# Operands of the down projection issued five steps ahead in program order, across changes of product

## The chip, the cores and the metric

The kernel runs on one core of a Trainium2 chip. The metric is the device time of one execution in microseconds (us); the time of a kernel is the median of its timed runs. The profile is of one further execution, whose own time and span are given beside it.

## What is computed

One layer of a hybrid decoder on x of 2048 tokens by 1024 channels, in fp32: a normalised input projection feeds a short convolution and a state-space mixer, an output projection adds their result to x, and an MLP follows. The change touches only the last product of the MLP:

```python
h = _rmsnorm(x, norm_mlp_pre[i])
f = jnp.square(jax.nn.relu(jnp.einsum("btd,df->btf", h, w_up[i])))    # 1024 -> 4096
f = jnp.einsum("btf,fd->btd", f, w_down[i])                           # 4096 -> 1024
x = x + _rmsnorm(f, norm_mlp_post[i])
```

## The kernel before

Every fp32 operand of a matmul is split into a high and a low part, and a product is made of three matmuls: high by high, high by low, low by high. `split` (L495, L496) does this: ACT casts the high part, DVE subtracts it for the low one.

The down projection (`down_stage`) is done in the manner of Strassen: seven products of block sums instead of eight of blocks, in the order 0, 1, 5, 6, 4, 2, 3. Below, "5.3" is step 3 of product 5. Each product runs over 16 steps p of the inner dimension. A step multiplies one tile of weights (128x512) with eight tiles of activations, at eight *sites* (two groups g, four token tiles t). Each site has one PSUM bank, three named "mm" and five "ax", and there are eight banks in all. A step is therefore 8 x 3 = 24 matmuls (L826 to L828), and the first matmul of a product at a site needs the bank that the product before still holds there.

`down_operands(i, p)` issues what a step needs. On SP it loads one to three tiles of w_down into "raw" (L747) or the stored t2 (L744); `less` subtracts them on DVE into "us" (L734); for product 5, whose weight has three parts, the result is also stored to t2 (L753), for product 3 to read. `split` makes "wh" and "wl" of it. For each of the two groups it loads one or two parts of the activations from DRAM into "xt" (L760); where there are two, POOL subtracts them into "fs" (L734, the same helper). `split` puts the high parts into "hh" and "hl" and the low parts into seven homes that are used in turn ("row", "m" for group 0, "bk", "bT", "cT", "scm", "xd", "xdh" for group 1). Buffers: raw 6, us 4, xt 6, fs 4, wh and wl 9 each.

After the 16 steps, `close` takes a product's result out of its banks: an ACT copy for product 0 (L799), an add on DVE for the others (`add`, L791). For products 1, 2 and 3 `half` (ACT square L766, POOL multiply L768, DVE multiply L772) and `finish` (L776 to L783) follow with the normalisation, the sum with x and the store of the output. In the last product the last six steps are kept back and done site by site (LATE).

The program text issues the operands of a step right ahead of the matmuls of that step; the operands of 5.0 so come behind the closes of product 1 in the text. A scheduler of the framework then sets each engine's order, with the place in the text as priority, so that loads and casts run ahead of the text where their buffers allow. An engine works off its own list in order and waits at the head of it.

Of the kernel before, what the change touches and what calls it, by code (L numbers as in the profile page):

```python
# [44 lines left out]
def hybrid_layer(ctx: ExitStack, tc: tile.TileContext, x, xT, w_in, w_dt, w_out, w_up, w_down,  # L45
                 chan, rows, hrow, out):
    nc = tc.nc
    V, S, G, PE, SY = nc.vector, nc.scalar, nc.gpsimd, nc.tensor, nc.sync
# [5 lines left out]
    def big(tag, dt=F32):  # L54
        return sb.tile([P, 512], dt, tag=tag, name=tag, bufs=BUFS.get(tag, 1))

    def bank(tag="ax"):
        return ps.tile([P, 512], F32, tag=tag, name=tag, bufs=BUFS[tag])
# [4 lines left out]
    def cols(n, *dims):  # L63
        size = n
        for d in dims:
            size *= d
        a = cst[:, used[0]:used[0] + size]
        used[0] += size
        assert used[0] <= C_ALL
        return a.rearrange("p (a b) -> p a b", a=n) if dims else a  # L70
# [401 lines left out]
    NP = FF // P // 2  # L472
    NG = T // PB
    B7 = range(7)
    ORDER = (0, 1, 5, 6, 4, 2, 3)
# [3 lines left out]
    t2_d = [dram.tile([P, 512], F32, name=f"t2_{p}") for p in range(NP)]  # L479
# [13 lines left out]
    def split(v, tags):  # L493
        hi, lo = (big(t, F32R) for t in tags)
        S.copy(hi, v)  # L495
        V.tensor_sub(lo, v, hi.bitcast(F32))  # L496
        return hi, lo
# [223 lines left out]
        save("a12", relu2(plus(u3, product(3))), S)  # L721


    LATE = 6
    ROUND = (HOMES[0], HOMES[2][:7]), (HOMES[1], HOMES[3][:7])
    step = [0]

# [4 lines left out]
    def less(eng, tag, a, b):  # L732
        c = big(tag)
        eng.tensor_tensor(c, a, b, op=ALU.subtract)  # L734
        return c

    def down_operands(i, p):
        n = step[0]
        step[0] += 1
        ws = []  # L740
        for at in W_PARTS[i]:
            raw = big("raw")
            if at is None:
                SY.dma_start(raw, t2_d[p])  # L744
            else:
                j, k = at
                SY.dma_start(raw.rearrange("p (a b) -> p a b", a=1),  # L747
                             w_down[2 * p + j][:, k:k + 1, :])
            ws.append(raw)
        v = ws[0] if len(ws) == 1 else less(V, "us", ws[0], ws[1])  # L750
        if len(ws) == 3:
            v = less(V, "us", ws[2], v)
            S.dma_start(t2_d[p], v)  # L753
        w = split(v, ("wh", "wl"))
        f = []
        for g in range(NG):
            fs = []
            for part in F_PARTS[i]:
                fs.append(big("xt"))
                SY.dma_start(fs[-1], f_d[g][p][part])  # L760
            v = fs[0] if len(fs) == 1 else less(G, "fs", *fs)
            f.append(split(v, [r[n % len(r)] for r in ROUND[g]]))
        return f, w

    def half(m, s2, i, first=False):
        S.activation(big("us"), m, AF.Square, accum_out=s2[:, i:i + 1])  # L766
        if first:
            G.tensor_tensor(m, m, gmlp[i], op=ALU.mult)  # L768
            V.tensor_scalar(s2[:, 2:3], s2[:, i:i + 1], 1.0 / D, EPS, op0=ALU.mult, op1=ALU.add)
            return m  # L770
        v = big("fs")
        V.tensor_tensor(v, m, gmlp[i], op=ALU.mult)  # L772
        V.tensor_scalar(s2[:, 3:4], s2[:, i:i + 1], 1.0 / D, s2[:, 2:3], op0=ALU.mult, op1=ALU.add)
        return v

    def finish(m, s2, tok, last):  # L776
        r = cols(1)
        G.tensor_tensor(r, s2[:, 3:4], mhalf[:, :1], op=ALU.pow)
        for i in range(2):
            xt = big("raw" if last else "fs")  # L780
            SY.dma_start(xt, x1_d[tok][:, i * 512:(i + 1) * 512])
            V.scalar_tensor_tensor(xt, m[i], r, xt, op0=ALU.mult, op1=ALU.add)
            (SY if last and i == 0 else S if last else G).dma_start(out[tok * P:(tok + 1) * P, i * 512:(i + 1) * 512], xt)  # L783

    def down_stage():
        sites = [(g, t) for g in range(NG) for t in range(TT)]
        u, w, c, s2 = {}, {}, {}, {}

        def add(dst, a, pt):
            dst = big("acc") if dst is None else dst  # L790
            V.tensor_tensor(dst, a, pt, op=ALU.add)  # L791
            return dst

        def close(i, k, pt):
            g, t = k
            tok = 2 * g * TT + t
            if i == 0:
                u[k] = big("acc")
                S.copy(u[k], pt)  # L799
            elif i == 1:  # L800
                c[k] = add(None, u[k], pt)
                s2[k] = cols(4)
                half(c[k], s2[k], 0, True)
            elif i == 5:
                add(u[k], u[k], pt)
            elif i == 6:
                w[k] = add(None, u[k], pt)
            elif i == 4:
                u[k] = add(u[k], u[k], pt), add(None, w[k], pt)
            elif i == 2:  # L810
                add(u[k][0], u[k][0], pt)
                finish([c[k], half(u[k][0], s2[k], 1)], s2[k], tok, False)
                s2[k] = cols(4)
                half(u[k][1], s2[k], 1, True)
            else:
                add(w[k], w[k], pt)
                finish([half(w[k], s2[k], 0), u[k][1]], s2[k], tok + TT, True)

        for i in ORDER:
            late = LATE if i == ORDER[-1] else 0  # L820
            banks = {k: bank("mm" if n < 3 else "ax") for n, k in enumerate(sites)}

            def mac(p, ops, k):
                (fh, fl), (wh, wl) = ops[0][k[0]], ops[1]
                ts = slice(k[1] * P, (k[1] + 1) * P)
                PE.matmul(banks[k], lhsT=fh[:, ts], rhs=wh, start=(p == 0), stop=False)  # L826
                PE.matmul(banks[k], lhsT=fh[:, ts], rhs=wl, start=False, stop=False)  # L827
                PE.matmul(banks[k], lhsT=fl[:, ts], rhs=wh, start=False, stop=(p == NP - 1))  # L828

            kept = []  # L830
            for p in range(NP):
                ops = down_operands(i, p)
                if p >= NP - late:
                    kept.append((p, ops))
                    continue
                for k in sites:
                    mac(p, ops, k)
                    if p == NP - 1:
                        close(i, k, banks[k])
            for k in sites if kept else ():  # L840
                for p, ops in kept:
                    mac(p, ops, k)
                close(i, k, banks[k])

    raw = up_load(0, 0)
    for g in range(NG):
        hb7 = hidden_blocks(g)
        for p in range(NP):
# [3 lines left out]
            up(g, p, hb7, wb7)  # L852
            drain(1)
    down_stage()


# [39 lines left out]
```

## Time and profile before

| | us |
|---|---|
| timed runs | 2795.24, 2800.82, 2802.17 |
| median | 2800.82 |
| profiled execution | 2797.18 |
| its span | 2795.5 |
| PE busy in it | 2717.7 |

The mean granted clock of TensorE in the profiled execution is 0.987. The span is the time from the first to the last instruction in the trace; 1.7 us of the execution lie outside it. Engines are named PE (matmuls), PEld (weight loads of PE), DVE, ACT, POOL and SP; L826 is line 826 of the kernel. In a timeline, "[8.15 <-ACT wh L495]" says that the engine had stood idle for 8.15 us and that ACT's write of wh in line 495 released it. Records of adjacent matmuls overlap: a matmul of 0.39 us is followed by the next after 0.23.

### The profile page before, as it was taken

What the parts mean: (1) busy time and instruction counts of PE and PEld (TensorE: products, weight loads), DVE (VectorE), ACT (ScalarE), POOL (GpSimd) and SP (SyncE); (2) the same over time, 40 slices, a digit from 0 to 9 for tenths busy, and PEclk for the clock granted to TensorE, in tenths of its full rate; (3) what the DMA queues carried; (4) which work ended last, traced back from release to release, by engine and by line L of the source; (5) the groups of instructions that cost most, each with busy time, mean ns of one, the idle gap of its engine ahead of it and who ended that gap; (6) DMA issues with size and microseconds to landing.
All of it is one profiled execution on the core that took longest, in us unless ns stands there. A gap on an engine that the chain in (4) does not pass through costs nothing.

```text
span 2795.5 us, 37710 instructions
## 1 busy us (share of the span) xinstructions
PE 2717.7 (97%) x12822; PEld 2239.3 (80%) x12822; DVE 1886.4 (67%) x3351; ACT 1353.3 (48%) x2361; POOL 645.3 (23%) x546
## 2 busy tenths in 40 slices
PE   8999999999999999999999999999999999799978
PEld 6888888888888888788887888878888877688867
DVE  6675867767676678677587776886665336665675
ACT  6545545464455455555554565665455323233331
POOL 1111312113221224221121233321221011413330
PEclk9999999999999999999999999999999999999989
DMA  8423334333344325643335556763436438866565
GB/s 276 141 87 117 107 112 147 123 110 98 117 137 139 112 97 182 215 153 113 109 100 168 175 186 213 272 216 140 147 121 222 143 121 293 281 240 215 189 218 186
DMA packets 257521, 456.83 MB, mean 163 GB/s; under 512 B 28080, under 2 KB 44848, under 8 KB 257328
## 3 DMA queue, kind: packets, MB, share of 16 engines
q1 hardware_dynamic: 199184, 361.60, 39.3%
q10 hardware_dynamic: 51744, 71.84, 7.0%
q0 software_dynamic: 6400, 20.98, 1.9%
q8 instruction: 101, 1.65, 0.2%
q14 instruction: 92, 0.75, 0.1%
HBM read 359.81 MB, written 94.50 MB: 163 GB/s over the span
## 4 chain that ended last, share of the span: by engine, by line
PE 55%; DVE 2%; DMA 2%; issue 0%; ACT 0%; POOL 0%; SPq 0%; ACTq 0%; DVEq 0%; POOLq 0%
PE ax L827 4%; PE ax L826 4%; PE ax L828 4%; PE mm L686 3%; PE mm L687 3%; PE mm L688 3%; PE ax L686 3%; PE ax L687 3%; PE ax L688 3%; PE mm L827 3%; PE mm L828 3%; PE mm L826 3%; PE mm L155 3%; PE mm L154 3%; PE mm L156 3%; PE ax L166 1%
## 5 line engine op out<-in xcount | busy, mean ns | idle before, releaser
L154 PE MATMUL mm<-hh,wh 128*128 128x512 f32 x1408 | 555.5, 395 | 4.2 <-ACT hh L143 2.2
L155 PE MATMUL mm<-hl,wh 128*128 128x512 f32 x1408 | 551.0, 391 | 0.6 <-DVE hl L144 0.5
L156 PE MATMUL mm<-hh,wl 128*128 128x512 f32 x1408 | 550.1, 391 | 0.0
L99 DVE TENSOR_TENSOR wl<-raw,wh 128x512 fp32r<-128x512 f32 x480 | 368.2, 778 | 240.6 <-ACT wh L98 229.3
L98 ACT CAST wh<-raw 128x512 fp32r<-128x512 f32 x480 | 293.0, 617 | 464.5 <-PE mm L155 294.4
L154 PEld LDWEIGHTS mm<-hh,wh 128*128 128x128 f32 x1408 | 265.6, 189 | 59.8 <-issue 3.3
L156 PEld LDWEIGHTS mm<-hh,wl 128*128 128x128 f32 x1408 | 265.4, 189 | 55.8
L155 PEld LDWEIGHTS mm<-hl,wh 128*128 128x128 f32 x1408 | 265.5, 189 | 55.4 <-DVE hl L144 2.0
L166 PE MATMUL ax<-wh,yh 128*128 128x512 f32 x512 | 201.1, 393 | 0.0
L168 PE MATMUL ax<-wh,yl 128*128 128x512 f32 x512 | 199.5, 390 | 0.0
L167 PE MATMUL ax<-wl,yh 128*128 128x512 f32 x512 | 199.3, 389 | 0.0
L496 DVE TENSOR_TENSOR wl<-us,wh 128x512 fp32r<-128x512 f32 x192 | 148.5, 777 | 72.5 <-ACT wh L495 42.9
L495 ACT CAST wh<-us 128x512 fp32r<-128x512 f32 x192 | 114.8, 617 | 129.3 <-DVE us L734 60.5
L826 PE MATMUL ax<-wh,hl 128*128 128x512 f32 x448 | 175.0, 391 | 0.0
L827 PE MATMUL ax<-wl,hl 128*128 128x512 f32 x448 | 174.6, 390 | 0.0
L826 PE MATMUL mm<-wh,hh 128*128 128x512 f32 x336 | 132.5, 397 | 39.8 <-ACT wh L495 25.4
L496 DVE TENSOR_TENSOR wl<-raw,wh 128x512 fp32r<-128x512 f32 x99 | 83.4, 846 | 102.3 <-ACT wh L495 59.6
L734 POOL TENSOR_TENSOR fs<-xt 128x512 f32<-128x512 f32 x64 | 94.8, 1489 | 226.5 <-DMA xt<-f_a 94.7
L717 POOL TENSOR_TENSOR fs<-uc 128x512 f32<-128x512 f32 x32 | 42.2, 1320 | 398.3 <-ACT uc L698 203.9
L827 PE MATMUL mm<-wl,hh 128*128 128x512 f32 x336 | 132.8, 395 | 0.7 <-DVE wl L496 0.7
L369 POOL TENSOR_TENSOR row<-row,cT 128x512 f32<-128x512 f32 x60 | 98.9, 1669 | 133.7 <-ACT cT L295 78.0
L697 ACT ACTIVATE uc<-uc 128x512 f32<-128x512 f32 x128 | 80.7, 631 | 101.2 <-DVE uc L693 91.5
(462 smaller groups left out, 6009.3 us busy)
## 6 DMA issues: line engine op xcount, KB each, us to landing
raw<-w_in_dram SPq DMA_DIRECT2D x352, 256.0 KB, 2.8
xt<-f_a SPq DMA_DIRECT2D x192, 256.0 KB, 4.5
raw<-w_down_dram SPq DMA_DIRECT2D x176, 256.0 KB, 4.9
raw<-w_out_dram SPq DMA_DIRECT2D x128, 256.0 KB, 2.8
f_a<-uc ACTq DMA_DIRECT2D x128, 256.0 KB, 2.2
xt<-f_s SPq DMA_DIRECT2D x96, 256.0 KB, 4.1
raw<-w_up_dram SPq DMA_DIRECT2D x68, 256.0 KB, 3.4
row<-cs SPq DMA_DIRECT2D x64, 256.0 KB, 3.9
```

What stands on the lines that cost most here:

```text
L98: S.copy(hi, raw)
L99: V.tensor_sub(lo, raw, hi.bitcast(F32))
L154: PE.matmul(pt, lhsT=wh[:, ks], rhs=ah[k], start=(k == 0), stop=False)
L155: PE.matmul(pt, lhsT=wh[:, ks], rhs=al[k], start=False, stop=False)
L156: PE.matmul(pt, lhsT=wl[:, ks], rhs=ah[k], start=False, stop=(k == KT - 1))
L166: PE.matmul(pts[t], lhsT=a, rhs=wh, start=(i == 0), stop=False)
L167: PE.matmul(pts[t], lhsT=a, rhs=wl, start=False, stop=False)
L168: PE.matmul(pts[t], lhsT=c, rhs=wh, start=False, stop=(i == n - 1))
L496: V.tensor_sub(lo, v, hi.bitcast(F32))
L826: PE.matmul(banks[k], lhsT=fh[:, ts], rhs=wh, start=(p == 0), stop=False)
L827: PE.matmul(banks[k], lhsT=fh[:, ts], rhs=wl, start=False, stop=False)
L828: PE.matmul(banks[k], lhsT=fl[:, ts], rhs=wh, start=False, stop=(p == NP - 1))
```

## The change

A list of all steps in the order of the products is made ahead, and `ready` holds the operands that have been issued. Before the matmuls of a step are issued, operands are issued until six steps (AHEAD + 1) are in `ready`; the step then takes the oldest. So the operands of a step now stand in the text five steps of matmuls earlier, and those of a product's first five steps stand ahead of the closes of the product before. The store of t2 goes from ACT's queue to POOL's. The whole diff:

```diff
--- before.py
+++ after.py
@@ -721,7 +721,7 @@
         save("a12", relu2(plus(u3, product(3))), S)
 
 
-    LATE = 6
+    LATE, AHEAD = 6, 5
     ROUND = (HOMES[0], HOMES[2][:7]), (HOMES[1], HOMES[3][:7])
     step = [0]
 
@@ -750,7 +750,7 @@
         v = ws[0] if len(ws) == 1 else less(V, "us", ws[0], ws[1])
         if len(ws) == 3:
             v = less(V, "us", ws[2], v)
-            S.dma_start(t2_d[p], v)
+            G.dma_start(t2_d[p], v)
         w = split(v, ("wh", "wl"))
         f = []
         for g in range(NG):
@@ -816,6 +816,8 @@
                 add(w[k], w[k], pt)
                 finish([half(w[k], s2[k], 0), u[k][1]], s2[k], tok + TT, True)
 
+        order = [(i, p) for i in ORDER for p in range(NP)]
+        ready = []
         for i in ORDER:
             late = LATE if i == ORDER[-1] else 0
             banks = {k: bank("mm" if n < 3 else "ax") for n, k in enumerate(sites)}
@@ -829,7 +831,9 @@
 
             kept = []
             for p in range(NP):
-                ops = down_operands(i, p)
+                while order and len(ready) <= AHEAD:
+                    ready.append(down_operands(*order.pop(0)))
+                ops = ready.pop(0)
                 if p >= NP - late:
                     kept.append((p, ops))
                     continue
```

Nothing is computed otherwise; the number of loads, subtractions, casts and matmuls is the same. What changes is each engine's order. Three places are shown; a number behind a name counts the tiles of the program, so that the same step has another number before and after.

**DVE at the end of product 1, before.** acc_21709 to acc_21772 are the eight closes of product 1, row_22059 and bT_22065 low parts of activations of product 5, us_21792 the first subtraction for the weight of 5.0.

```order
L496 TENSOR_TENSOR row_22059<-xt_22056,hh_22058 128x512
L496 TENSOR_TENSOR bT_22065<-xt_22062,hl_22064 128x512
L791 TENSOR_TENSOR acc_21709<-acc_21013,mm_21050 128x512
...
L791 TENSOR_TENSOR acc_21772<-acc_21048,ax_21057 128x512
...
L496 TENSOR_TENSOR row_22110<-xt_22107,hh_22109 128x512
...
L734 TENSOR_TENSOR us_21792<-raw_21786,raw_21788 128x512
```

**The same place after the change.** us_21822 and wl_21826 are the weight of 5.4, us_21927 the first subtraction for 5.5; acc_21844 to acc_21907 are the closes.

```order
L734 TENSOR_TENSOR us_21822<-raw_21818,us_21820 128x512
...
L496 TENSOR_TENSOR wl_21775<-us_21771,wh_21774 128x512
L496 TENSOR_TENSOR xdh_21736<-xt_21733,hl_21735 128x512
L496 TENSOR_TENSOR wl_21826<-us_21822,wh_21825 128x512
...
L791 TENSOR_TENSOR acc_21844<-acc_21103,mm_21140 128x512
...
L791 TENSOR_TENSOR acc_21907<-acc_21138,ax_21147 128x512
...
L496 TENSOR_TENSOR row_21990<-xt_21987,hh_21989 128x512
...
L734 TENSOR_TENSOR us_21927<-raw_21921,raw_21923 128x512
```

The weights of 5.0 to 5.4 have moved from behind the closes of product 1 to ahead of them.

**DVE at the end of product 5, before.** us_23000 is the weight of 6.7, us_23054 that of 6.8; acc_21013 and so on are the closes of product 5.

```order
L496 TENSOR_TENSOR wl_22949<-us_22946,wh_22948 128x512
L734 TENSOR_TENSOR us_23000<-raw_22996,raw_22998 128x512
L496 TENSOR_TENSOR m_22959<-fs_22956,hh_22958 128x512
L734 TENSOR_TENSOR us_23054<-raw_23050,raw_23052 128x512
L496 TENSOR_TENSOR scm_22915<-fs_22912,hl_22914 128x512
L791 TENSOR_TENSOR acc_21013<-acc_21013,mm_21778 128x512
L496 TENSOR_TENSOR wl_23003<-us_23000,wh_23002 128x512
L791 TENSOR_TENSOR acc_21018<-acc_21018,mm_21779 128x512
```

**The same place after the change.** us_22934 is the weight of 6.8, us_22988 that of 6.9, us_23042 that of 6.10.

```order
L734 TENSOR_TENSOR us_22934<-raw_22930,raw_22932 128x512
L496 TENSOR_TENSOR wl_22775<-us_22772,wh_22774 128x512
L496 TENSOR_TENSOR row_22715<-fs_22712,hh_22714 128x512
L496 TENSOR_TENSOR m_22785<-fs_22782,hh_22784 128x512
L734 TENSOR_TENSOR us_22988<-raw_22984,raw_22986 128x512
L496 TENSOR_TENSOR cT_22725<-fs_22722,hl_22724 128x512
L496 TENSOR_TENSOR wl_22829<-us_22826,wh_22828 128x512
L496 TENSOR_TENSOR m_22839<-fs_22836,hh_22838 128x512
L496 TENSOR_TENSOR scm_22795<-fs_22792,hl_22794 128x512
L734 TENSOR_TENSOR us_23042<-raw_23038,raw_23040 128x512
L791 TENSOR_TENSOR acc_21103<-acc_21103,mm_21913 128x512
```

The closes of product 5 now stand behind the subtraction of 6.10, two steps further back than before.

**SP at this place, before.** raw_23050 and raw_23052 are the two weight tiles of 6.8, xt_23016 and xt_23018 parts of 6.7, xt_23060 to xt_23072 the four parts of 6.8.

```order
L760 DMA xt_23018<-f1_7_a21_241 128x512
L747 DMA raw_23050<-w_down_dram 128x512
L747 DMA raw_23052<-w_down_dram 128x512
L760 DMA xt_23060<-f0_8_a11_149 128x512
L760 DMA xt_23062<-f0_8_a21_151 128x512
L760 DMA xt_23070<-f1_8_a11_245 128x512
L760 DMA xt_23072<-f1_8_a21_247 128x512
L747 DMA raw_23104<-w_down_dram 128x512
```

**SP after the change.** raw_23038 and raw_23040 are the weight tiles of 6.10, xt_22896 and xt_22898 parts of 6.7, xt_22940 to xt_22952 the four parts of 6.8.

```order
L747 DMA raw_23038<-w_down_dram 128x512
L760 DMA xt_22896<-f1_7_a11_239 128x512
L760 DMA xt_22898<-f1_7_a21_241 128x512
L760 DMA xt_22940<-f0_8_a11_149 128x512
L760 DMA xt_22942<-f0_8_a21_151 128x512
L760 DMA xt_22950<-f1_8_a11_245 128x512
L760 DMA xt_22952<-f1_8_a21_247 128x512
L747 DMA raw_23040<-w_down_dram 128x512
L747 DMA raw_23092<-w_down_dram 128x512
```

The second weight tile of 6.10, on which the closes now wait, stands behind the four parts of 6.8; before, both weight tiles of 6.8 stood ahead of them.

**DVE at the end of product 2, before.** acc_21013 to acc_21048 are the closes of product 2, us_25238 is the weight of 3.0.

```order
L496 TENSOR_TENSOR cT_25483<-xt_25480,hl_25482 128x512
L791 TENSOR_TENSOR acc_21013<-acc_21013,mm_24266 128x512
...
L791 TENSOR_TENSOR acc_21048<-acc_21048,ax_24273 128x512
...
L734 TENSOR_TENSOR us_25238<-raw_25234,raw_25236 128x512
L769 TENSOR_SCALAR cst_63<-cst_63 128x1
L734 TENSOR_TENSOR us_25284<-raw_25280,raw_25282 128x512
```

**The same place after the change.** us_24958 and wl_24961 are the weight of 3.0, wl_25145 is of 3.4, us_25348 of 3.5; acc_21103 to acc_21138 are the closes.

```order
L734 TENSOR_TENSOR us_24958<-raw_24954,raw_24956 128x512
...
L496 TENSOR_TENSOR wl_24961<-us_24958,wh_24960 128x512
...
L496 TENSOR_TENSOR wl_25145<-us_25142,wh_25144 128x512
...
L791 TENSOR_TENSOR acc_21103<-acc_21103,mm_24396 128x512
...
L791 TENSOR_TENSOR acc_21138<-acc_21138,ax_24403 128x512
...
L734 TENSOR_TENSOR us_25348<-raw_25344,raw_25346 128x512
```

The weights of 3.0 to 3.4 have moved ahead of the closes of product 2; the one of 3.5 stands where 3.0 stood.

## Rows read from the trace of the kernel before

**Rows 1.** The page, section 1: busy time of each engine.

```profile
PE 2717.7 (97%) x12822; PEld 2239.3 (80%) x12822; DVE 1886.4 (67%) x3351; ACT 1353.3 (48%) x2361; POOL 645.3 (23%) x546
```

**Rows 2.** Windows, PE: stretch, its length, PE busy, granted clock, DMA share, GB/s.

```profile
2127.00:2200.00 73.00, 73.00 (x324) 1.00 0.62 213
2297.00:2318.00 21.00, 12.15 (x38) 0.67 0.26 78
```

**Rows 3.** Timeline of PE, product 1 to 5: start, us, instruction, idle before and releaser.

```profile
2290.59 0.39 PE L826 MATMUL mm<-wh,hh 128*128 128x512 f32 x1
...
2296.03 0.39 PE L826 MATMUL mm<-wh,hh 128*128 128x512 f32 x1
...
2309.78 1.65 PE L826 MATMUL mm<-wh,hh 128*128 128x512 f32 x3 [8.15 <-ACT wh L495]
...
2319.70 0.40 PE L826 MATMUL mm<-wh,hh 128*128 128x512 f32 x1
```

**Rows 4.** Timeline of PE, product 5 to 6.

```profile
2395.87 0.39 PE L826 MATMUL mm<-wh,hh 128*128 128x512 f32 x1
...
2401.08 0.39 PE L828 MATMUL ax<-wh,xd 128*128 128x512 f32 x1
2415.79 0.77 PE L826 MATMUL mm<-wh,hh 128*128 128x512 f32 x1 [14.32 <-DVE acc L791]
...
2423.42 0.39 PE L826 MATMUL mm<-wh,hh 128*128 128x512 f32 x1
```

**Rows 5.** Timeline of PE, product 2 to 3.

```profile
2673.66 0.39 PE L826 MATMUL mm<-wh,hh 128*128 128x512 f32 x1
...
2678.87 0.39 PE L828 MATMUL ax<-wh,scm 128*128 128x512 f32 x1
2696.54 0.80 PE L826 MATMUL mm<-wh,hh 128*128 128x512 f32 x1 [17.29 <-ACT wh L495]
...
2703.95 0.39 PE L826 MATMUL mm<-wh,hh 128*128 128x512 f32 x1
```

**Rows 6.** Timeline of DVE behind the end of product 1.

```profile
2301.67 0.69 DVE L791 TENSOR_TENSOR acc<-acc,ax 128x512 f32<-128x512 f32 x1
...
2304.01 1.68 DVE L734 TENSOR_TENSOR us<-raw 128x512 f32<-128x512 f32 x1
```

**Rows 7.** Timeline of DVE around the end of product 5.

```profile
2369.86 0.69 DVE L734 TENSOR_TENSOR us<-raw 128x512 f32<-128x512 f32 x1 [1.85 <-DMA raw<-w_down_dram]
...
2403.72 0.69 DVE L734 TENSOR_TENSOR us<-raw 128x512 f32<-128x512 f32 x1 [4.75 <-DMA raw<-w_down_dram]
...
2413.75 0.69 DVE L734 TENSOR_TENSOR us<-raw 128x512 f32<-128x512 f32 x1 [3.50 <-DMA raw<-w_down_dram]
...
2414.96 0.68 DVE L791 TENSOR_TENSOR acc<-acc,mm 128x512 f32<-128x512 f32 x1
```

**Rows 8.** Timeline of DVE behind the end of product 2.

```profile
2683.59 0.67 DVE L791 TENSOR_TENSOR acc<-acc,ax 128x512 f32<-128x512 f32 x1
...
2691.78 4.00 DVE L734 TENSOR_TENSOR us<-raw 128x512 f32<-128x512 f32 x1
```

**Rows 9.** Windows, all engines: length, busy PE to POOL, granted clock, DMA share, GB/s.

```profile
2318.00:2340.00 22.00, 22.00 (x99) 18.17 (x98) 17.51 (x28) 7.06 (x12) 0.00 (x0) 1.00 0.99 357
2380.00:2400.00 20.00, 20.00 (x90) 16.57 (x89) 10.97 (x12) 5.59 (x9) 9.88 (x7) 1.00 0.69 237
```

**Rows 10.** DMA issues: output and input, queue, count, size, median us to landing.

```profile
f_s<-fs POOLq DMA_DIRECT2D x64, 256.0 KB, 3.2
...
t<-us ACTq DMA_DIRECT2D x16, 256.0 KB, 5.1
```

**Rows 11.** Timeline of POOL, end of the up stage to product 6.

```profile
2130.92 1.09 POOL L702 DMA_DIRECT2D f_s<-fs  x2
2298.44 11.71 POOL L768 TENSOR_TENSOR acc<-acc,gain 128x512 f32<-128x512 f32 x8 [166.42 <-ACT us L766]
...
2365.35 1.29 POOL L734 TENSOR_TENSOR fs<-xt 128x512 f32<-128x512 f32 x1 [55.19 <-DMA xt<-f_a]
```

## The prediction

> **What bounds the kernel now.** The page comes first: PE is busy for 2717.7 of 2795.5 us [rows 1], so only the time in which PE stands still, or is clocked lower, can be won. The table by windows then shows where that time lies in the last third: in a normal stretch of the down stage (2127 to 2200 us) PE is busy throughout at a granted clock of 1.00, while around 2297 to 2318 us it is busy for 12.15 of 21 us at a clock of 0.67 [rows 2]. The timeline of PE gives three such places, each at a change of product. The reader is to see two things in it: the release named behind the gap, and what the change of product costs from a matmul before it to one behind it. A step of 24 matmuls takes 2296.03 - 2290.59 = 5.44 us [rows 3], so two undisturbed steps take 10.88.
>
> - A, product 1 to 5: 2319.70 - 2296.03 = 23.67, so 12.79 us are lost [rows 3].
> - B, product 5 to 6: 2423.42 - 2395.87 = 27.55, so 16.67 us are lost [rows 4].
> - C, product 2 to 3: 2703.95 - 2673.66 = 30.29, so 19.41 us are lost [rows 5].
>
> Together that is 48.9 us, the lower clock after each gap included; the other three changes of product lose nothing. The timeline of DVE says why. At A the subtraction for the first weight of product 5 (L734, 2304.01) stands behind the eight closing adds of product 1, the last of them at 2301.67 [rows 6], and PE waits for the cast made from it [rows 3]. C is the same with more behind the adds: last add at 2683.59, first subtraction for product 3 at 2691.78 [rows 8]. B is of another kind. PE waits there for a closing add [rows 4], and that add stands on DVE behind the subtractions of weights of steps 6.5 to 6.8, which wait for their loads; the one of 6.8 ran at 2413.75 and the first add at 2414.96 [rows 7], although product 5's first banks had been complete since before 2401.08 [rows 4].
>
> **The change part by part.** No matmul, cast, subtraction or load is added or taken away. What moves is the order.
>
> *A goes: 12.8 us.* In the new order on DVE the subtractions and low parts of the weights of 5.0 to 5.4 stand ahead of the first closing add, and 5.5 is the first behind it. Five steps of PE are 5 x 5.44 = 27 us of cover for 5.5; before, its counterpart (5.0) had its subtraction 2304.01 - 2301.67 = 2.3 us behind the last add [rows 6]. Their loads fall into product 1, which has room: 213 GB/s in its window [rows 2], against the 357 that product 5 reaches [rows 9].
>
> *C goes but for half a microsecond: 18.9 us.* The weights of 3.0 to 3.4 stand ahead of the closing adds. What is late next is the last closing add itself: in the trace it ended at 2683.59 + 0.67 = 2684.3 [rows 8], and PE, started at 2679.1 right behind its last matmul [rows 5], would ask for that bank seven sites of 0.68 us later, at 2683.9. That leaves about 0.5 us. The weight of 3.5 comes at about 13 us behind the product's end, as 3.0 did [rows 5, 8], and is asked for at 27.
>
> *B stays and grows by 3.3 us.* This term decides the number. PE ends product 5 earlier by A: 2401.3 - 12.8 = 2388.5. In the new order the closing adds stand behind the subtraction of 6.10 instead of 6.8, and on SP the second weight of 6.10 stands behind all four loads of parts of 6.8. How late is it? Before, the subtraction of 6.1 ran at 2369.86 and the one of 6.8 at 2413.75 [rows 7]: 6.27 us per step. The floor is what the DMA engines move: six loads of 256 KB are 1.57 MB, at the 357 GB/s seen when they were 99% busy [rows 9] 4.4 us. I take 6.1 at 2360, 10 us earlier: less than PE's 12.8, since the first 20 us of product 5 are already at the ceiling of rows 9. For the nine steps to 6.10 I take 4.9 us each: the last steps before 6.8 ran 5.0 apart (2403.72 to 2413.75 for two) [rows 7], and the new order of SP has fewer points at which a load of parts waits for POOL. That is an estimate. It gives 2360 + 44.1 = 2404.1. From the subtraction of 6.8 to PE's start it took 2415.79 - 2413.75 = 2.04 us [rows 4, 7], so PE starts at 2406.1, after 17.6 us, and the low clock behind the gap adds 16.67 - 14.32 = 2.35: a loss of 20.0 instead of 16.7. At the floor (2360 + 39.6) the loss is 15.5, at the old pace (2360 + 56.4) 32.3; both ends are kept for the range.
>
> *The sixteen stores of t2 cost nothing.* They leave ACT for POOL. POOL issues such a store in 1.09 / 2 = 0.55 us, so 8.8 us in all, and it has nothing to do for 166.42 us before product 1's closes and for 55.19 us before its first subtraction of product 6 [rows 11]. If that cover were gone, 8.8 us of POOL would delay the parts of product 6, behind a weight that is late anyway. Nobody reads t2 before product 3. But a store holds its "us" buffer until it has landed, and four buffers are two steps. From ACT a t2 store took 5.1 us, and the only other stores of this size and pattern from POOL, f_s, took 3.2 [rows 10]; two steps have 10.88.
> The Trainium skill speaks against this part: the page "SBUF — State Buffer", section "SBUF: two separate sides", says that a DMA issued from GpSimd has its descriptors written by that engine and can starve while DVE holds the port pair that both share, and advises ACT or SP as issuer. The 3.2 us of rows 10 do not show that here; by that rule the term would be the last of the rivals below, by the rows it is nothing.
>
> Sum: -12.8 - 18.9 + 3.3 = -28.4. The profiled execution took 2797.2 us and its span 2795.5, so 1.7 lie around the span; the result is 2768.8. The three timed runs were 2795.24, 2800.82 and 2802.17, so the median is 3.6 above the profiled one; I say 2769.
>
> **The rivals.**
> - *B disappears too.* For it: the weight of 6.1 was there 30 us before product 5 ended [rows 4, 7], and product 5 and 6 together need less than their 174 us of DMA time, so five steps of lead could carry the loads past the change. Against it: from 2380 to 2400 the DMA engines were busy for 0.69 only [rows 9], so the loads waited for buffers and not for the engines, and the closes were moved back behind two more steps. Time: 2797.2 - 48.4 = 2749; with a rest of 10 us, 2759.
> - *A or C is only exchanged for another wait*, for instance because 5.5's weight, behind eight adds and eight multiplications on POOL, is not there in 27 us, or because PE waits for buffers of the parts. Half of A or C staying is 6 to 10 us on top: 2775 to 2779, and up to 2784 with B slower than forecast. Against it speak the 27 us.
> - *The order is moved but PE's gaps are not*, as when the loads of 5.0 to 5.4 and 3.0 to 3.4 come no earlier on the chip: the time stays within 0.3% of before, 2792 to 2809. Against it: at A and C PE's release is not a DMA [rows 3, 5].
> - *Slower than before: the t2 stores hold "us".* If a store from POOL lands after T us, two steps of product 5 take at least T + 1.9 (two subtractions and the issue, 0.69 + 0.69 + 0.55 [rows 7, 11]) instead of 10.88. Some 11 steps lie behind the lead, 5.5 pairs, so PE loses 5.5 x (T - 9.0) - 27. That eats the 28.4 won from T = 19 us on; at T = 25 it loses 61 and the time is 2830. Against it: 3.2 us for f_s, and 19 us is nearly four times what a t2 store took from ACT [rows 10].
> By the two times that the same page of the Trainium skill gives in the section "A bandwidth-pool intuition that's wrong (but worth ruling out)" (about 620 ns alone, about 3100 beside a DVE copy) the 5.1 us would become an estimated 25; its own text on which DVE operations do this names copies rather than two-input operations, and no run here shows it.
>
> **How the numbers follow.** Forecast, A and C gone and B between 15.5 and 32.3: 0.62, times 2764 to 2781. B down to 10 us or less: 0.20, 2749 to 2759. A or C half exchanged: 0.11, up to 2784. Unchanged: 0.04. Slower: 0.03. A measurement of this kernel can tell 0.3% from no change, which is 8.4 us; the first three cases are beyond it, so faster is 0.93, the same 0.04, slower 0.03. The range from 2750 to 2784 leaves out the fringe of the second case and the last two.
>
> **What would show it.** Right: no idle time on PE at the end of product 1 (now near 2301 us) and under 1 us at the end of product 2, with the granted clock at 1.00 there; at the end of product 5 a gap of 13 to 28 us released by an add of L791, with a subtraction L734 that waited for a load of a weight right ahead of it on DVE; t2 stores that land in under 9 us. Wrong: PE runs through the end of product 5, or it stops at A or C with another release, or new idle time shows inside product 5 behind L734 waiting for a store of t2.

## The result, and the profile after

| | before | after |
|---|---|---|
| median, us | 2800.47 (4 runs) | 2764.11 (4 runs, 2758.75 to 2769.65) |
| ratio, with 95% interval | | 0.9873 [0.985, 0.9897] |
| profiled execution, us | 2797.18 | 2764.97 |
| its span, us | 2795.5 | 2763.3 |

The change is worth 36.4 us by the medians; 2769 was forecast, with a range from 2750 to 2784. One execution of the kernel e3 below took 11355 us, four times the others, and no ratio counts it. The page of the changed kernel, answering to [rows 1]; the line below it has the granted clock in 40 equal slices of the span, in tenths of full speed (9 is 90% or more):

```profile
PE 2711.4 (98%) x12822; PEld 2234.2 (81%) x12822; DVE 1891.5 (68%) x3351; ACT 1352.1 (49%) x2361; POOL 656.8 (24%) x562
...
PEclk9999999999999999999999999999999999999999
```

PE does the same matmuls in a span 32.2 us shorter: it is busy for 98% instead of 97%. The lines of the matmuls are now L828 to L830.

The timeline of PE at the three changes of product, first A (product 1 to 5), to be read against [rows 3]:

```profile
2300.47 0.39 PE L828 MATMUL mm<-wh,hh 128*128 128x512 f32 x1
...
2305.91 0.39 PE L828 MATMUL mm<-wh,hh 128*128 128x512 f32 x1
...
2311.35 0.39 PE L828 MATMUL mm<-wh,hh 128*128 128x512 f32 x1
```

The first matmuls of 1.15, 5.0 and 5.1 are 5.44 us apart each. A is gone: 2311.35 - 2300.47 - 10.88 = 0.00, where 12.79 were lost. B, product 5 to 6, against [rows 4]:

```profile
2387.51 0.39 PE L828 MATMUL mm<-wh,hh 128*128 128x512 f32 x1
...
2392.72 0.39 PE L830 MATMUL ax<-wh,xd 128*128 128x512 f32 x1
2400.94 0.77 PE L828 MATMUL mm<-wh,hh 128*128 128x512 f32 x1 [7.83 <-DVE acc L791]
...
2408.51 0.39 PE L828 MATMUL mm<-wh,hh 128*128 128x512 f32 x1
```

The gap is still there and its release is the same, a closing add, but it is 7.83 us instead of 14.32. The loss is 2408.51 - 2387.51 - 10.88 = 10.12, where 16.67 were lost. C, product 2 to 3, against [rows 5]:

```profile
2658.75 0.39 PE L828 MATMUL mm<-wh,hh 128*128 128x512 f32 x1
...
2664.19 0.39 PE L828 MATMUL mm<-wh,hh 128*128 128x512 f32 x1
...
2667.61 0.47 PE L828 MATMUL ax<-wh,hl 128*128 128x512 f32 x1 [0.54 <-DVE acc L791]
...
2670.43 0.39 PE L828 MATMUL mm<-wh,hh 128*128 128x512 f32 x1
```

The loss is 2670.43 - 2658.75 - 10.88 = 0.80, where 19.41 were lost; the 0.54 us in it are spent waiting for a closing add. The windows over A and over C, with the columns of [rows 2], have the granted clock at 1.00 where [rows 2] had 0.67 around A:

```profile
2300.47:2322.47 22.00, 22.00 (x99) 1.00 0.41 143
2658.75:2679.75 21.00, 20.46 (x91) 1.00 0.49 164
```

Together 12.79 + 6.55 + 18.61 = 37.95 us. The down stage, from its first matmul to its last, took 2785.32 - 2127.39 = 657.93 us before and 2751.81 - 2131.83 = 619.98 after, which is also 37.95 less. So the whole gain lies at these three places. The span fell by 5.8 less than that mainly because the stage began 4.4 us later in this execution, behind code that the change leaves alone; in the thirteen kernels of this study, which share that code, the start lies between 2126.6 and 2135.6 us. The three without a lead lie at the low end (up to 2128.5), three with one lie there too; one execution of each does not tell whether the lead costs something there. Below, losses are therefore counted in the stage.

### The profile page after: what moved, and what is told of

Read it like the earlier page. It is cut to its first block, busy times and chain, and to the rows that moved or that the text cites. A ratio compares the mean times of both kernels' runs of the same rounds, so it can differ in the third digit from the quotient of the medians.

```text
span 2763.3 us, 37736 instructions
## 1 busy us (share of the span) xinstructions
PE 2711.4 (98%) x12822; PEld 2234.2 (81%) x12822; DVE 1891.5 (68%) x3351; ACT 1352.1 (49%) x2361; POOL 656.8 (24%) x562
## 4 chain that ended last, share of the span: by engine, by line
PE 53%; DMA 3%; DVE 1%; ACT 1%; issue 1%; POOL 0%; ACTq 0%; DVEq 0%; SPq 0%; POOLq 0%
PE ax L828 4%; PE ax L829 4%; PE ax L830 4%; PE ax L686 3%; PE mm L687 3%; PE mm L686 3%; PE ax L688 3%; PE mm L688 3%; PE ax L687 3%; PE mm L828 3%; PE mm L829 3%; PE mm L830 3%; PE mm L155 3%; PE mm L156 3%; PE mm L154 3%; PE ax L166 1%
## 5 line engine op out<-in xcount | busy, mean ns | idle before, releaser
L828 PE MATMUL ax<-wh,hl 128*128 128x512 f32 x448 | 174.4, 389 | 0.5 <-DVE acc L791 0.5
L828 PE MATMUL mm<-wh,hh 128*128 128x512 f32 x336 | 131.6, 392 | 7.8 <-DVE acc L791 7.8
```

## The experiments

Each loss is counted as above. "Stage" is from its first matmul to its last in the profiled execution, and the total loss is what it has over 609.05: that is 609.85 of the run e7 below less the 0.80 which e7 loses at C. What lies at none of the places shown is put to the product it is in.

| kernel | lead | A and in product 5 | B | C and in product 3 | stage | median, ratio [95%] |
|---|---|---|---|---|---|---|
| before | 0 | 12.8 | 16.7 | 19.4 | 657.93 | |
| the change | 5 | 0 | 10.1 | 0.8 | 619.98 | 2764.1, 0.9873 [0.985, 0.9897] |
| e1 | 5 | 0 | 12.4 | 0.8 | 622.28 | 2763.8, 0.9868 [0.9851, 0.9884] |
| e2 | 0 | 12.8 | 13.7 | 20.7 | 656.34 | 2798.0, 0.9992 [0.9982, 1.0002] |
| e3 | 1 | 7.3 | 17.4 | 14.0 | 647.72 | 2791.6, 0.9965 [0.9955, 0.9975] |
| e8 | 2 | 0 | 20.6 | 11.2 | 640.91 | 2782.6, 0.9934 [0.9916, 0.9952] |
| e9 | 8 | 0 | 0 | 2.1 | 611.97 | 2755.0, 0.9848 [0.9832, 0.9864] |
| e10 | 5 at A only | 0 | 10.7 | 19.8 | 639.57 | 2781.0, 0.9941 [0.9926, 0.9956] |
| e11 | 5, not at A | 11.8 | 11.9 | 0.8 | 633.60 | 2777.4, 0.9929 [0.9912, 0.9946] |
| e4 | 5, seven weights | 0 | 7.1 | 1.2 | 617.31 | 2761.5, 0.9864 [0.985, 0.9879] |
| e5 | 5, parts on DVE | 0 | 8.7 | 0.8 | 618.55 | 2760.7, 0.9852 [0.9836, 0.9869] |
| e6 | 0, parts on DVE | 12.8 | 2.9 | 19.5 | 644.23 | 2790.2, 0.9952 [0.9937, 0.9968] |
| e7 | 5, both of these | 0 | 0 | 0.8 | 609.85 | 2755.5, 0.9829 [0.9813, 0.9846] |

**The two halves of the change: e1 and e2.** e1 keeps the lead and gives the t2 stores back to ACT; e2 moves the stores and has no lead.

```diff
 e1
-            G.dma_start(t2_d[p], v)
+            S.dma_start(t2_d[p], v)
 e2
-    LATE, AHEAD = 6, 5
+    LATE, AHEAD = 6, 0
```

> The lead of five steps alone; the t2 stores stay on ACT. Losses at the changes of product are counted as in the prediction (first matmul of the last step to first matmul of the second step, less 10.88 us); the changed kernel lost 0 at A (1 to 5), 10.1 at B (5 to 6), 0.8 at C (2 to 3). Theory 'order on DVE': the store plays no part, so A 0, B 8 to 12, C 1, time 2760 to 2769. Rival 'the stores': part of the gain, that of B above all, comes from taking 16 stores off ACT, which casts every high part; then B is back near 16.7 and the time near 2770 to 2775.

> The t2 stores alone on POOL, no lead. Theory 'order on DVE': A 12.8, B 16.7, C 19.4 as before, each within 1.5, time 2795 to 2803. Rival 'the stores': B falls by 5 or more and the time by as much. Second rival, the one against the change (a store from POOL holds its buffer): L734 of product 5 waits for stores, A or B grows, landing time of t2 above 9 us.

e1 measures what the change measures (its B, 12.4, is just above the 8 to 12 expected), e2 what the kernel before does: its interval holds 1. In the time, the stores play no part that can be told from nothing. At B they may play a small one: with the stores on POOL B is lower in both pairs, by 2.3 us (the change against e1) and by 2.9 (e2 against before, where 1.5 at most was expected). There is one trace of each kernel, so how much B varies between executions of one kernel is not known, and these two differences can be read either way. Where a run below has its stores on POOL and no lead, e2 and not the kernel before is what to hold it against. The t2 stores issued from POOL landed about as those from ACT had (5.1 us in [rows 10], 4.3 in e1); DMA issues of the changed kernel:

```profile
t<-us POOLq DMA_DIRECT2D x16, 256.0 KB, 5.2
```

**The length of the lead: e3, e8, e9.** Only AHEAD differs from the change.

```diff
-    LATE, AHEAD = 6, 5
+    LATE, AHEAD = 6, 1      e3; 2 in e8, 8 in e9
```

> AHEAD = 1 instead of 5, so that only the weight of 5.0 and of 3.0 stands ahead of the closes, and the closes of product 5 stand behind 6.7. Theory 'order on DVE' (a step's weight must stand ahead of the closes or have its cover in steps): at C the weight of 3.1 comes 13 to 17 us behind the end of product 2 and is asked for after 5.44, so C loses 9 to 13; A loses 2 to 5 (5.1 comes 8 to 10 behind the end); B 8 to 15. Time 2775 to 2785. Rival 'any lead will do' (only the first step's weight was late): A 0, C 1, time 2760 to 2769.

> AHEAD = 2: weights of 5.0, 5.1, 3.0 and 3.1 ahead of the closes. With a lead of 1 the idle time was 4.3 us at A and 11.0 at C, without lead 8.8 and 17.3, with five 0 and 0.5. Theory 'the first weight behind the closes must be covered by the steps ahead of it': each further step of lead takes off 5.44 to 6.3 us, so A 0 and C 4 to 6; B 9 to 14; time 2773 to 2783. Rival 'a lead works all or nothing' (it is the loads' start that counts): A and C as with 1, or 0.

What PE waited for in e3, from 2200 us on (engine, line, releaser: us in total, times, longest):

```profile
PE mm L828 <- DVE acc L791: 14.3, 1, 14.3
PE mm L828 <- ACT wh L495: 13.8, 2, 11.0
PE mm L829 <- DVE wl L496: 1.6, 1, 1.6
PE ax L828 <- DVE acc L791: 0.6, 1, 0.6
```

A lead of one is not enough at A or C: the release is again ACT's wh, now of the step behind the one that was led. With a lead of two A is gone and C still waits 5.64 us for wh. So "any lead will do" fell. But the theory's numbers missed too: e3 lost more than expected at all three places and took 6.6 us more than the top of its range, and e8, whose time is just inside its own, lost 20.6 us at B where I had said 9 to 14, and 11.2 at C where I had said 4 to 6. Part of what A gave up came back at B: with two steps of lead PE reaches the end of product 5 12.8 us earlier than before, and its gap there is 17.70 us instead of 14.32. Of the leads tried so far, only five makes B shrink. A and B together show it better than each alone: 29.5, 24.7, 20.6 and 10.1 us for a lead of 0, 1, 2 and 5. The windows over product 1 tell what goes along with this (columns as in [rows 2]), each from the first matmul of the product to about its last. In the kernel before:

```profile
2214.60:2301.50 86.90, 86.90 (x384) 1.00 0.41 137
```

With a lead of two (e8):

```profile
2215.00:2302.00 87.00, 87.00 (x385) 1.00 0.49 167
```

In the change, a lead of five:

```profile
2218.90:2305.90 87.00, 87.00 (x385) 1.00 0.58 198
```

With a lead of eight (e9):

```profile
2222.70:2309.70 87.00, 87.00 (x386) 1.00 0.65 227
```

Over 87 us, 137 and 198 GB/s differ by 5.3 MB. Counted by landing in the trace, most of it is 13 more loads of product 5 (46 instead of 33 land before product 1 ends), 3.4 MB, and five of the t2 stores, 1.3 MB; the lead of two has 39 of the loads there, the lead of eight 54. These transfers are made in product 1, where the DMA engines have room, and products 5 and 6 no longer have to ask for them. At the 357 GB/s of [rows 9] the 5.3 MB are worth 15 us, the loads alone 9.5; both are estimates. This became the theory "head start", and e9 was its test.

> AHEAD = 8. With leads of 0, 1, 2 and 5 the losses of A, of product 5 and of B together were 29.5, 24.6, 20.6 and 10.1 us, about 3.9 less for a step of lead. Theory 'head start': what is loaded ahead in product 1 is not asked of the DMA engines in products 5 and 6, so three more steps take off up to 10 us, B 0 to 4, time 2752 to 2760. Rival 'buffers end it': seven homes of parts and nine weights allow no more to be made ready than a lead of five already does; B 8 to 12, time as with a lead of five, 2760 to 2769.

B is gone altogether, and the rival with it. The waits of PE in e9:

```profile
PE mm L828 <- DVE acc L791: 1.8, 1, 1.8
PE ax L828 <- DVE acc L791: 0.5, 1, 0.5
```

The median is 9 us below that of the change and the stage 8.0 shorter; the intervals of the two ratios still overlap a little, so the times alone do not quite separate them. What the longer lead costs is 2.1 us at the end of product 2, 1.8 of them waiting for an add, and 0.75 at the change 4 to 2.

**Where the lead is needed: e10 and e11.**

```diff
-                while order and len(ready) <= AHEAD:
+                while order and len(ready) <= (AHEAD if i in (0, 1) else 0):    e10
+                while order and len(ready) <= (0 if i in (0, 1) else AHEAD):    e11
```

> The lead of five only while products 0 and 1 are issued, so that it carries over the change 1 to 5 and is then used up; none at 5 to 6 and 2 to 3. Theory 'head start': A 0, B 8 to 12 as with the full lead, because what B gained comes from the loads made in product 1; C 19.4 as before; time 2779 to 2787. Rival 'the lead at 5 to 6 is what shortens B': B 17 or more, time 2787 to 2795.

> The lead of five only from product 5 on, none at 1 to 5. Theory 'head start': A 12.8 and B 14 to 18 as before, C 0.8; time 2778 to 2786. Rival 'the lead at 5 to 6 is what shortens B': B 10 or less, time 2769 to 2777. With the run before this one, the gains at A with B and at C should add up to those of the full lead.

e10 settles it for the head start: with a lead over the first change alone A and B together lose 10.7, against 10.1 with the full lead and 26.5 in e2, and C is 19.8, as without. The loads say the same: 46 of product 5 land before product 1 ends, as in the change. e11 gave neither of the two answers clean: B is 11.9, below the 14 to 18 expected, though A kept its loss of 11.8. Like e10, it has the stores on POOL, and e2, which differs from it by the lead alone, has 13.7 at B. So a lead from product 5 on is worth 1.8 us at B, less than the 2.9 between e2 and before; whether it helps there at all stays open. Against e2 the parts nearly add up: e10 gains 16.8 us in the stage and e11 22.7, together 39.5, and the full lead 36.4.

**What DVE does ahead of the closes: e4 to e7.** The forecast said that B ends with a subtraction that waits for its load. The changed kernel's timeline of DVE shows such waits up to the weight of 6.4 and none from there to the closes; the weights of 6.1, 6.3, 6.4 and 6.10 and the first closing adds, against [rows 7]:

```profile
2355.64 0.69 DVE L734 TENSOR_TENSOR us<-raw 128x512 f32<-128x512 f32 x1 [2.05 <-DMA raw<-w_down_dram]
...
2369.80 0.69 DVE L734 TENSOR_TENSOR us<-raw 128x512 f32<-128x512 f32 x1 [5.08 <-DMA raw<-w_down_dram]
...
2374.64 0.69 DVE L734 TENSOR_TENSOR us<-raw 128x512 f32<-128x512 f32 x1 [1.86 <-DMA raw<-w_down_dram]
...
2398.45 1.74 DVE L734 TENSOR_TENSOR us<-raw 128x512 f32<-128x512 f32 x1
2400.12 1.27 DVE L791 TENSOR_TENSOR acc<-acc,mm 128x512 f32<-128x512 f32 x2
```

The window ahead of it, columns as in [rows 9]:

```profile
2380.00:2400.00 20.00, 13.11 (x58) 10.51 (x56) 20.00 (x16) 6.46 (x11) 15.31 (x10) 0.96 0.99 362
```

DVE was busy for all 20.00 us. Its operation took 1.74 us where the same one took 0.69 before. POOL was busy for 15.31 us of that stretch, subtracting parts, and the DMA engines for 0.99 of it, where they had been for 0.69 before [rows 9]. So the place of the closes, DVE's slow pace or the loads could be the cause. e4 puts the closes behind 6.8 instead of 6.10, by seven weight buffers; e5 takes POOL's work to DVE; e6 does that to the kernel before; e7 does both.

```diff
 e4, e7
-        w = split(v, ("wh", "wl"))
+        w = split(v, (f"wh{n % 7}", f"wl{n % 7}"))
 e5, e6, e7
-            v = fs[0] if len(fs) == 1 else less(G, "fs", *fs)
+            v = fs[0] if len(fs) == 1 else less(V, "fs", *fs)
```

> The changed kernel, but the down stage's wh and wl are rings of seven tiles instead of nine, which makes the scheduler put the closes of product 5 behind the subtraction of 6.8 instead of 6.10. In the changed kernel 6.8 was subtracted 5 us before product 5 ended, 6.10 at 5.7 us behind it. Theory 'the closes stand behind a weight that lands late': B falls from 10.1 to 0 to 3, A and C as they are, time 2753 to 2760. Rival 'product 6 is late as a whole' (its loads and POOL's subtractions, whatever stands where): B stays at 7 or more, or the time lost there shows up again inside product 6 as a wait for parts or weights; time 2760 to 2769. A third case: seven weights are too few and PE waits for ACT's wh inside the products; time above 2769.

e4 came out as its rival had said, if barely: B is 7.1, not 0 to 3, and the median 2761.5. The place of the closes alone is thus not what makes B. The timeline of DVE in e4, from the subtraction of 6.8 on:

```profile
2391.36 1.75 DVE L734 TENSOR_TENSOR us<-raw 128x512 f32<-128x512 f32 x1
2393.04 1.75 DVE L496 TENSOR_TENSOR m<-fs,hh 128x512 fp32r<-128x512 f32 x1
2394.71 1.74 DVE L496 TENSOR_TENSOR scm<-fs,hl 128x512 fp32r<-128x512 f32 x1
2396.37 0.68 DVE L791 TENSOR_TENSOR acc<-acc,mm 128x512 f32<-128x512 f32 x1
```

No row has a wait; three operations of 1.75 us stand ahead of the first add, and PE had ended product 5 at 2391.7.

> The changed kernel, with the 64 subtractions of activation parts in products 6 and 2 (L734, fs) on DVE instead of POOL. In the changed kernel DVE worked without a pause for the 20 us ahead of the closes of product 5, its two-input operations took 1.75 us while POOL subtracted and 0.68 when it did not, and the weight of 6.10 had landed 2.9 us before DVE came to it. Theory 'DVE is slowed by POOL': with POOL idle every such operation takes 0.68, a step of product 6 is 6 x 0.6 = 3.6 us of DVE instead of 4 x 1.7 = 6.8, and the idle gap at B falls from 7.8 to 0 to 3 us; time 2753 to 2760. Rival 'the loads are late' (the forecast's reason): the operations are shorter but DVE now waits for loads of w_down or of parts ahead of the closes, gap 6 or more, time 2762 to 2768. Third case: DVE, with 64 more operations, is itself late elsewhere; time above 2768.

> The kernel before (no lead, t2 stores on ACT) with the same 64 subtractions on DVE. Theory 'DVE is slowed by POOL': B's gap of 14.3 us falls by 6 or more, A and C stay at 8 and 17 us idle; time 2785 to 2794. Rival 'the loads are late': SP's loads waited for POOL's subtractions, which DVE now does in the same places; B within 3 of 14.3, time 2796 to 2803.

> Both together: parts subtracted on DVE and seven weights, so that the closes of product 5 stand behind 6.8. Theory 'DVE is slowed by POOL, and the closes stand behind late work': no gap at B over 1 us, 0.5 at C; time 2750 to 2757, below both kernels. Rival 'the loads are late': gap of 3 or more with a load as what DVE waited for.

e5 did to the operations what was expected and hardly anything to the gap. Its timeline of DVE, from the subtraction of 6.8 to that of 6.10 and the first add:

```profile
2385.52 0.69 DVE L734 TENSOR_TENSOR us<-raw 128x512 f32<-128x512 f32 x1 [2.95 <-DMA raw<-w_down_dram]
...
2392.15 0.68 DVE L734 TENSOR_TENSOR us<-raw 128x512 f32<-128x512 f32 x1
...
2394.56 0.68 DVE L791 TENSOR_TENSOR acc<-acc,mm 128x512 f32<-128x512 f32 x1
```

And of PE behind it:

```profile
2395.38 0.77 PE L828 MATMUL mm<-wh,hh 128*128 128x512 f32 x1 [6.37 <-DVE acc L791]
```

Everything takes 0.68 or 0.69 now, but DVE stands for 2.95 us for a load of 6.8, and the gap is 6.37. Its median, 2760.7, lies between the two ranges, but the gap and the wait are those of the rival: the theory that POOL's slowing of DVE alone makes B in the changed kernel falls. With DVE fast, it is the loads that are late. In e7 DVE is fast and the closes stand behind two steps less. The first closing add in its timeline of DVE:

```profile
2393.94 0.68 DVE L791 TENSOR_TENSOR acc<-acc,mm 128x512 f32<-128x512 f32 x1
```

That is before product 5 ends (2390.15 for the first matmul of 5.15, and 5.44: 2395.6), and the gap is gone. All that PE waits for in e7 from 2200 us on:

```profile
PE ax L828 <- DVE acc L791: 0.5, 1, 0.5
```

e7's interval lies below that of the change. What e4 and e5 could not do alone (7.1 and 8.7 left at B), the two do together.

e6 went as the theory had said: without any lead, B falls to 2.9 there, by 13.8 us, where in e5 it fell by 1.5. PE comes to B 12.8 us later than with the lead, and the waits of SP give a second reason. A load of a part waits until the subtraction of an earlier part has freed its "xt" buffer. These waits, from the first matmul of product 5 to that of product 6, in the kernel before, in e6, in the change and in e5 (waiting line, releaser: us in total, times, longest):

```profile
SPq L760 <- POOL fs L734: 23.6, 8, 4.4
SPq L760 <- DVE fs L734: 9.6, 7, 2.1
SPq L760 <- POOL fs L734: 7.5, 5, 2.3
SPq L760 <- DVE fs L734: 11.3, 6, 3.3
```

Without a lead SP loses 23.6 us to POOL's subtractions, and moving them to DVE takes 14.0 of these away; with the lead only 7.5 are left, and the move adds to them. That fits the difference between e6 and e5; no run tries it apart. A and C stay at 12.8 and 19.5 in e6. This does not say that the pace of DVE plays no part there, for e6 leaves POOL's multiplications (L768) in place, and the first subtraction for product 3 takes in e6 what it took in [rows 8]:

```profile
2679.14 4.01 DVE L734 TENSOR_TENSOR us<-raw 128x512 f32<-128x512 f32 x1
```

e7 and e9 both have medians about 9 us under the change's; the difference between them is not resolved, and the two were not tried together.

## Why the prediction was right, point by point

**What bounds the kernel.** Right. The gain of the stage is the sum of the three losses, to 0.01 us.

**A, 12.8.** Right: 12.79. One reading in it was wrong, to no harm: the 213 GB/s taken for product 1 belong to a window in product 0 (2127 to 2200), and product 1, from 2214.4 on, moved 137. It had more room than was counted. e3 and e8 show that the weights ahead of the closes must give enough steps of cover for the first one behind them: one step does not, two do.

**C, 18.9.** Right: 18.61. The rest is the last closing adds, as worked out. The timeline of DVE, against [rows 8]:

```profile
2668.73 0.68 DVE L791 TENSOR_TENSOR acc<-acc,ax 128x512 f32<-128x512 f32 x1
...
2677.01 4.06 DVE L734 TENSOR_TENSOR us<-raw 128x512 f32<-128x512 f32 x1
```

The subtraction of 3.5 came 12.8 us behind the end of product 2 (2677.01 - 2664.19), and 13 was forecast; nothing waited for it.

**B, 3.3 worse.** This term was mis-sized: B got better by 6.55, so the term was off by 9.9 us. The step that failed is "I take 6.1 at 2360, 10 us earlier: less than PE's 12.8". The other steps of the term held as numbers: from 6.1 to 6.10 DVE took (2398.45 - 2355.64) / 9 = 4.76 us a step, where 4.9 was taken, and from the last subtraction to PE 2.5 us, where 2.04 was taken. But the subtraction of 6.1 came 49.7 us behind the start of product 5 (2355.64 - 2305.91) where the forecast had put it at 2360 - 2301.5 = 58.5. I had used the room in product 1 for A and not for B: what is moved there is 5.3 MB, an estimated 15 us of DMA time, off the account of the stretch that I called "already at the ceiling". In the change the first 22 us of product 5 are not at the ceiling: the DMA engines move 152 GB/s there and come near the 357 only from 2340 us on. The windows, columns as in [rows 9]:

```profile
2305.91:2327.91 22.00, 22.00 (x99) 18.22 (x98) 21.92 (x32) 9.38 (x19) 12.09 (x12) 1.00 0.45 152
2340.00:2360.00 20.00, 20.00 (x90) 16.57 (x89) 12.16 (x19) 6.91 (x13) 5.03 (x6) 1.00 0.97 354
```

The wait named there also differed, so the agreement of 4.76 with 4.9 is in part luck. Up to 6.4 DVE is late by loads, as forecast, and behind that by its own work, slowed by POOL; the forecast knew only loads. By the sign set for being right, a gap of 13 to 28 us with a wait for a load right ahead of it, B was not as forecast.

**The stores, nothing.** Right by the times of e1 and e2, with the 2.3 and 2.9 us at B left open. The rival in which they hold "us" did not come about: 5.2 us, where 19 would have been needed. The starving of DMAs issued from GpSimd that the Trainium skill describes ("SBUF — State Buffer", section "SBUF: two separate sides") is tied there to a mode of DVE that copies use, and is not seen here for stores beside two-input operations of DVE.

**The time.** The case given 0.62 was B between 15.5 and 32.3, with 2764 to 2781; B was 10.1, and the time of 2764.11 lies at the edge of that case by luck. The profiled execution came out at 2764.97 for a forecast of 2768.8 because two misses partly cancelled: B was 9.9 better than forecast, and 5.8 us were lost outside the stage; the rest, 0.3, is C.

**The rivals.** That B disappears was given 0.20, and the truth lay at its edge. Its mechanism, that the lead carries the loads past the change, is the one at work, and at a lead of eight it goes all the way. That B grows as PE comes earlier is what a lead of two did (20.6, near the 20.0 forecast for five).

## What to carry to other kernels

When one gap is closed, the next one meets an engine that comes earlier by that much: sum the gaps that share a resource, here the loads of products 5 and 6, and count what the edit takes off that resource in a stretch that has room. A lead has to be long enough for both, for the first step behind the blocking work and for the transfers after it, and the shortest lead that closes the first gap (two steps here) may hand part of its gain back at the next. An in-order engine that closes one phase should not have work of the next phase ahead of it that can be late, whether it is late by a load or by its own pace.

## What the hardware showed that was not expected

A two-input operation of DVE on 128x512 fp32 took 0.68 us with POOL idle and up to 1.78 while POOL ran subtractions of the same size; in e5, with these gone, those ahead of the closes of product 5 took 0.68 or 0.69. Where POOL worked without a pause, at the end of product 2, one took 4.06 us (the row 2677.01 above). The rule on this is in the Trainium skill, "SBUF — State Buffer", section "Who interferes with whom": a DVE instruction with two inputs in SBUF contends with a GpSimd instruction that reads SBUF. The trace agrees. Not every operation is hit: in the window ahead of the closes 16 of them took DVE's 20.00 us, 1.25 each, so four in a step cost 5.0 us, nearly the 5.44 of a step, while six at 0.68 cost 4.1. Moving POOL's share onto the busier engine was no loss.
